# Wider token-major products in a two-block transformer kernel: 512-column blocks, smaller weight granules, other buffer counts

## The chip, the cores and the metric

The kernel runs on one core of a Trainium2 chip. The metric is the device time in microseconds of one execution. Times are medians of several runs of the same program. One further execution was recorded by the hardware profiler; durations and waits in this document come from it.

## The reference

Two residual blocks over 1024 tokens of width 1024, in float32, one after the other. Cut to its products:

```python
# first block
proj = rmsnorm(x) @ w_in                    # 1024 x 9216: a_u, a_v, a_gate, q, k, v, b_gate, gates
y_a  = chunked_spatial_gating(gelu(a_u), gelu(a_v), ...) * silu(a_gate)
y_b  = dilated_attention(q, k, v) * silu(b_gate)
x    = rmsnorm(x + (g_a * (y_a @ w_proj_a) + g_b * (y_b @ w_proj_b)) @ w_out)
# second block, two layers
h = h + rms(ssd_scan(conv(u @ m_in ...)) * silu(z)) * y_g @ m_out     # Mamba-2 mixer, 2048 inner
h = h + (p_0 @ ple_proj) * sigmoid(rmsnorm(h) @ ple_gate)             # gated embedding
h = h + (stick_breaking_attention(q, k, v) * silu(gate)) @ s_out
h = h + (p_1 @ ple_proj) * sigmoid(rmsnorm(h) @ ple_gate)
```

## The kernel before

**Precision and layout.** Every large product is made of three float32r products: each operand is split into a rounded high part and a remainder, and hi x hi, hi x lo and lo x hi are summed in PSUM (`mm`, line 521). The activation of a stage lies transposed, channels on partitions, in an `Act` region (`act1`, `act2`). Its 1024 tokens are 8 token tiles of 128 (`NT`), its 1024 channels 8 channel tiles (`KT`).

**Two kinds of product.** `gemm_b` (line 548) is channel-major: a 128 x 128 tile of the weights is stationary and 512 tokens move; the result has output channels on partitions. `gemm_a` (line 587) is token-major: a 128 x 128 tile of the activation is stationary and the weights move; the result has tokens on partitions. The token-major products are the v projection of the first block (`av`, in `branch_a`), its output projection (`wo`, in `merge`), the four z products of the scan (`z`, in `mamba`), the two halves of the scan's output product (`mo`, in `mamba_out`), the two halves of the last output product (`so`, in `stick_out`) and, in a loop of its own, the gated embedding (`ple`, line 1932, twice), which multiplies each token tile by 8 channel tiles of the gate weights and 2 of the projection.

In `gemm_a` the columns are cut in blocks. For each block, for each token tile, for each channel tile k there are three matmuls into one PSUM bank; then the tile is evacuated by a function of the stage (`ev`, `ev_h`, `ev0`, `ev1`, `evz`).

**Weights.** `Job` (line 344) cuts a weight matrix into granules of 1024 elements per partition, 512 KB each: kind "a" 4 channel tiles x 256 columns, kind "b" 8 x 128, kind "c" 2 x 512. All granules of the kernel stand in one list in order of use. `Weights.loads` (line 383) loads each into a raw slot when one is free. `Weights.splits` (line 396) then takes a split slot, multiplies the granule on GpSimd by a gain where a norm's gain is folded in (`mo`, `ple`'s gate, the products of the second attention), makes the high part on ScalarE (on GpSimd once `hi_on_pool` is set, near the end of the second attention) and the remainder on GpSimd, and gives back the raw slot. A block gives back its split slots after its last token tile. `limit` (line 420) sets how many split and raw slots are in use: there are five split slots and two raw ones in all; a stage that needs the memory for something else uses fewer (four split at first, two in the attentions, there with one raw slot in the second). `taken` (line 969) raises the limit when a region has been given back. At the end `mamba_out` and `stick_out` add two more split slots (offsets 140 and 148).

**Order.** Streams of work (Python generators) are interleaved by a planner, `Sched` (line 245), that keeps an estimated clock of PE and of the other engines, and steps the stream of highest priority that is due. The result is a fixed order of instructions on every engine and DMA queue; at run time each engine follows its own order and waits on semaphores. A granule's ScalarE and GpSimd instructions stand in those queues at the place where the planner put them. All loads and stores are issued from SyncE's queue.

**Memory.** SBUF is one arena, cut by `CUTS` (line 73) into blocks that hold either float32 or float32r. Offsets are in KB per partition; names such as m24r or m172f in the profile give the block's offset and its kind.

**Other buffers that the change touches.** `partial` (line 1851) writes the first half of an output product to DRAM in pieces of 256 columns; `residual` adds them back. `evz` (line 1551) evacuates z with a Tanh on ScalarE and one vector operation, and stores it. `stick_out` hands out the loads of the residual in `begin_turn` (line 2159), one every `TURN[1]` tiles from tile `TURN[0]`.

## Time and profile before

| what | value |
|---|---|
| time, median of 3 runs | 3258.47 us (3257.03 to 3262.03) |
| the profiled execution's own time | 3255.16 us |
| its span in the profile | 3253.4 us |
| PE (TensorE) busy | 3102.3 us, 18830 matmuls |
| VectorE, ScalarE, GpSimd busy | 1725.7, 1404.9, 1257.3 us |
| HBM traffic | 89 GB/s over the span |

PE is the matmul engine, PEld its weight loads, DVE is VectorE, ACT ScalarE, POOL GpSimd, SP SyncE, on whose queue the DMAs are issued. Matmuls overlap, so that a matmul's own duration is longer than the distance between two of them; the distance is read from the starts in the timeline. "Idle before ... <- X" gives the time that an engine waited and the work that released it. L522 is the matmul in `mm`, L533 a transpose, L484 an ACT activation, L488 and L499 vector operations, L507 and L511 GpSimd operations: all are helpers, so the tiles' names tell the stage.

### The profile page before, as it was taken

What the parts mean: (1) busy time and instruction counts of PE and PEld (TensorE: products, weight loads), DVE (VectorE), ACT (ScalarE), POOL (GpSimd) and SP (SyncE); (2) the same over time, 40 slices, a digit from 0 to 9 for tenths busy, and PEclk for the clock granted to TensorE, in tenths of its full rate; (3) what the DMA queues carried; (4) which work ended last, traced back from release to release, by engine and by line L of the source; (5) the groups of instructions that cost most, each with busy time, mean ns of one, the idle gap of its engine ahead of it and who ended that gap; (6) DMA issues with size and microseconds to landing.
All of it is one profiled execution on the core that took longest, in us unless ns stands there. A gap on an engine that the chain in (4) does not pass through costs nothing. (4 is left out here: it accounts for less than half of the span.)

```text
span 3253.4 us, 47763 instructions
## 1 busy us (share of the span) xinstructions
PE 3102.3 (95%) x18830; PEld 2742.4 (84%) x18830; DVE 1725.7 (53%) x3080; ACT 1404.9 (43%) x2569; POOL 1257.3 (39%) x772
## 2 busy tenths in 40 slices
PE   8999999999999999999999989999998989998999
PEld 8988888888888789987878788899977778877899
DVE  2111146667673321567676765443457776878642
ACT  4322255556564311433232323223456766776421
POOL 3332111111112433324445454643335566657750
PEclk9999999999999999999999999999998999999999
DMA  4122221212122753322434334451201111113611
GB/s 138 52 68 78 81 68 57 63 53 59 53 66 91 258 175 130 113 74 77 113 83 114 81 102 146 137 205 40 85 22 33 41 38 40 40 41 120 238 55 52
DMA packets 296052, 291.33 MB, mean 90 GB/s; under 512 B 15556, under 2 KB 252276, under 8 KB 295828
## 3 DMA queue, kind: packets, MB, share of 16 engines
q1 hardware_dynamic: 295828, 288.29, 28.7%
q8 instruction: 147, 2.41, 0.3%
q14 instruction: 77, 0.63, 0.1%
HBM read 216.80 MB, written 71.43 MB: 89 GB/s over the span
## 5 line engine op out<-in xcount | busy, mean ns | idle before, releaser
L507 POOL TENSOR_TENSOR m8r<-m0f,m8r 128x1024 fp32r<-128x1024 f32 (+1 forms) x68 | 163.4, 2403 | 473.8 <-ACT m8r L484 419.1
L507 POOL TENSOR_TENSOR m16r<-m0f,m16r 128x1024 fp32r<-128x1024 f32 x66 | 167.0, 2530 | 440.6 <-ACT m16r L484 401.6
L488 DVE TENSOR_TENSOR m156r<-psum,m156r 128x384 fp32r<-128x384 f32 (+2 forms) x376 | 223.6, 605 | 157.9 <-ACT m156r L484 155.7
L484 ACT ACTIVATE m156r<-psum 128x384 fp32r<-128x384 f32 (+2 forms) x376 | 195.9, 534 | 197.1 <-PE psum L533 184.4
L507 POOL TENSOR_TENSOR m172f<-m172f,m24f 128x127 f32<-128x127 f32 (+7 forms) x128 | 185.0, 1455 | 155.8 <-DVE m24f L2039 106.1
L507 POOL TENSOR_TENSOR m24r<-m0f,m24r 128x1024 fp32r<-128x1024 f32 x64 | 155.8, 2438 | 215.6 <-ACT m24r L484 213.1
L2039 DVE TENSOR_TENSOR_SCAN m24f<-m24f,zero 128x128 f32<-128x128 f32 (+7 forms) x128 | 222.6, 1753 | 8.4 <-ACT m24f L484 7.9
L533 PE MATMUL psum<-ident,m172f 128*128 128x128 f32 (+1 forms) x1314 | 206.4, 280 | 21.5 <-DVE m172f L493 8.5
L499 DVE SCALAR_TENSOR_TENSOR m172f<-m172f,psum 128x256 f32<-128x256 f32 (+1 forms) x112 | 59.5, 534 | 267.8 <-ACT m172f L484 221.6
L533 PEld LDWEIGHTS psum<-ident,m172f 128*128 128x128 f32 (+1 forms) x1314 | 156.9, 144 | 41.4 <-DVE m172f L493 10.2
L484 ACT ACTIVATE m192f<-psum 64x256 f32<-64x256 f32 (+2 forms) x237 | 103.8, 438 | 199.6 <-PE psum L522 128.7
L507 POOL TENSOR_TENSOR smalls<-smalls,mhalf 128x1 f32<-128x1 f32 (+1 forms) x104 | 89.5, 864 | 163.9 <-DVE smalls L495 163.1
L522 PE MATMUL psum<-m108r 128*128 128x512 f32 (+3 forms) x384 | 141.7, 371 | 6.6 <-ACT m172f L484 4.5
L484 ACT ACTIVATE m40f<-psum 128x256 f32<-128x256 f32 (+1 forms) x150 | 66.5, 444 | 181.6 <-PE psum L522 141.6
L507 POOL TENSOR_TENSOR m0f<-m0f,cols 128x1024 f32<-128x1024 f32 x64 | 132.6, 2073 | 31.0 <-DMA m0f<-in_ple_gate_dram 12.6
L493 DVE TENSOR_SCALAR m172f<-m172f,smalls 128x512 f32<-128x512 f32 (+7 forms) x160 | 130.3, 814 | 19.7 <-POOL smalls L507 14.6
L1410 DVE CUSTOM_DVE_ANT_0 m172f<-psum,m24f 128x512 f32<-128x512 f32 (+1 forms) x192 | 102.8, 554 | 65.0 <-PE psum L522 64.8
L1418 ACT ACTIVATE m172f<-m172f,smalls 128x128 f32<-128x128 f32 (+7 forms) x128 | 99.3, 776 | 82.8 <-DVE smalls L495 81.2
L522 PE MATMUL psum<-m60r,m16r 128*128 128x512 f32 x504 | 134.8, 399 | 0.0
L522 PE MATMUL psum<-m44r,m8r 128*128 128x512 f32 x504 | 133.7, 399 | 0.7 <-DVE m108r L499 0.7
L522 PE MATMUL psum<-m60r,m8r 128*128 128x512 f32 x504 | 132.3, 397 | 1.7 <-DVE m108r L499 1.7
L522 PE MATMUL psum<-m44r,m16r 128*128 128x512 f32 x504 | 133.2, 402 | 0.0
(374 smaller groups left out, 8024.5 us busy)
## 6 DMA issues: line engine op xcount, KB each, us to landing
m0f<-in_w_in_dram SPq DMA_DIRECT2D x72, 512.0 KB, 3.8
m0f<-in_m_in_dram SPq DMA_DIRECT2D x38, 512.0 KB, 4.1
m92f<-acum SPq DMA_DIRECT2D x21, 512.0 KB, 10.4
m24f<-in_alibi_dram SPq DMA_DIRECT2D x16, 512.0 KB, 4.2
zd<-m40f SPq DMA_DIRECT2D x64, 128.0 KB, 1.9
m172f<-zd SPq DMA_DIRECT2D x32, 256.0 KB, 9.8
yd<-m172f SPq DMA_DIRECT2D x32, 256.0 KB, 2.2
m0f<-in_m_out_dram SPq DMA_DIRECT2D x16, 512.0 KB
```

Source lines behind the costliest of these rows:

```text
L484: self.nc.scalar.activation(out, in_, func, **k)
L488: self.nc.vector.tensor_tensor(out, a, b, op=op)
L493: self.nc.vector.tensor_scalar(out, a, s1, None, op0=op0)
L499: self.nc.vector.scalar_tensor_tensor(out, a, s, b, op0=op0, op1=op1)
L507: self.nc.gpsimd.tensor_tensor(out, a, b, op=op)
L522: self.nc.tensor.matmul(out, l, r, start=start, stop=stop)
L533: self.nc.tensor.transpose(out, in_, self.ident[:in_.shape[0], :in_.shape[0]])
L1410: nc.vector.tensor_tensor_reduce(row[:, k0:k0 + w], bank[:, :w], Tt[:, off + k0:off + k0 + w], 1.0, -3e38, op0=ALU.add, op1=ALU.max, accum ...
L1418: nc.scalar.activation(row[:, :n], row[:, :n], AF.Exp, bias=nm, accum_out=l)
L2039: nc.vector.tensor_tensor_scan(x[:, ::-1], x[:, ::-1], self.zero.to_broadcast([P, n]), 1.0, op0=ALU.mult, op1=ALU.add)
```

## The change

Token-major blocks become 512 columns wide, made of four granules of 2 channel tiles x 512 columns (kind "a"). The first z product, which carries 32 extra columns, keeps the old shape under the name "n". A split slot is given back as soon as the last token tile has used the granule, not at the end of the block. `ple` goes over 512 columns at a time and waits for each granule where it is first used. There is a sixth split slot (offset 200; 192 becomes the last) and a third raw slot (offset 208, a new cut of the arena); `limit` uses three raw slots unless told otherwise, the merge and the scan use five split slots and not four, the scan's output product six and not five. Evacuations, pieces and stores are 512 columns wide, with two slots where there were four of half the size; `TURN` is halved.

```diff
-    CUTS = (0, 8, 16, 24, 40, 44, 60, 76, 92, 108, 140, 156, 172, 192, 200, 216)
+    CUTS = (0, 8, 16, 24, 40, 44, 60, 76, 92, 108, 140, 156, 172, 192, 200, 208, 216)
...
-        nk, nc = {"a": (4, 256), "b": (KT, P), "c": (2, 512)}[kind]
+        nk, nc = {"n": (4, 256), "a": (2, 512), "b": (KT, P), "c": (2, 512)}[kind]
...
-    def limit(self, n, m=2):
+    def limit(self, n, m=3):
...
-        def products(gs, bank, t, ks):
+        def products(gs, bank, t, ks, over=False):
...
                 e = self.mm(ps, xl, g.hi[:, j, :], False, k == job.kt - 1)
+                if over and j == g.nk - 1:
+                    self.W.release(g)
             return e
...
-                e = yield from products(gs, bank, t, range(job.kt))
+                over = t == NT - 1
+                e = yield from products(gs, bank, t, range(job.kt), over)
...
-            for g in gs:
-                self.W.release(g)
...
-        self.W = Weights(self, self.res(0, 4, 2), Res([self.region(o, 8, "r") for o in (8, 16, 24, 32, 192)]))
+        self.W = Weights(self, Res([self.region(o, 4) for o in (0, 4, 208)]), Res([self.region(o, 8, "r") for o in (8, 16, 24, 32, 200, 192)]))
...
-                J["z", 0] = Job(self, m, 0, 512, "a", more=(5120, 32))
+                J["z", 0] = Job(self, m, 0, 512, "n", more=(5120, 32))
...
-                      go=self.taken(self.r2, 4))
+                      go=self.taken(self.r2, 5))
...
-        zo = self.res(40, 1, 4)
+        zo = self.res(40, 2, 2)
...
-        self.fill_y(self.act1, 1, self.res(172, 4, 3), [self.taken(self.r1, 5)] * NT)
-        ev0, begin, hp_tok = self.partial(self.hp, self.res(40, 1, 4))
+        self.fill_y(self.act1, 1, self.res(172, 4, 3), [self.taken(self.r1, 6)] * NT)
+        ev0, begin, hp_tok = self.partial(self.hp, self.res(40, 2, 2))
...
-        for cb in range(0, D, 256):
-            gs, (gp,) = self.J["pg", i, cb].blocks[0], self.J["pp", i, cb // 512 * 512].blocks[0]
-            pc = slice(cb % 512, cb % 512 + 256)
-            yield ([g.ready for g in gs], gp.ready)
+        for cb in range(0, D, 512):
+            gs, (gp,) = self.J["pg", i, cb].blocks[0], self.J["pp", i, cb].blocks[0]
...
-                    yield act.wait(k // 4, t * P, P)
+                    yield (act.wait(k // 4, t * P, P), gs[k // 2].ready)
...
+                    if j and t == NT - 1:
+                        self.W.release(g)
...
-    TURN = (16, 2)
+    TURN = (8, 1)
...
-        nj, es, half = self.res(172, 4, 2), self.res(188, 1, 4), {}
-        pact = self.embed(1, 156, es, self.weighed)
+        nj, es, half = self.res(172, 4, 2), Res([self.region(o, 2) for o in (188, 190, 212, 214)]), {}
+        pact = self.embed(1, 156, self.res(188, 1, 4), self.weighed)
```

## Rows read from the trace of the kernel before

**Rows 1.** The page's busy table and its 40 slices.
```profile
span 3253.4 us, 47763 instructions
...
PE 3102.3 (95%) x18830; PEld 2742.4 (84%) x18830; DVE 1725.7 (53%) x3080; ACT 1404.9 (43%) x2569; POOL 1257.3 (39%) x772
...
PE   8999999999999999999999989999998989998999
...
PEclk9999999999999999999999999999998999999999
```

**Rows 2.** Windows by stage: stretch, length, busy by engine, granted clock, DMA share, GB/s.
```profile
12.00:113.00 101.00, 99.15 (x801) 98.20 (x802) 25.91 (x44) 42.09 (x79) 29.32 (x22) 1.00 0.27 86
...
1252.00:1344.00 92.00, 92.00 (x770) 92.00 (x769) 26.33 (x54) 20.89 (x31) 24.30 (x18) 1.00 0.31 107
...
1400.00:1973.00 573.00, 531.33 (x3024) 453.80 (x3024) 393.99 (x572) 198.54 (x325) 272.03 (x179) 0.96 0.36 97
1973.00:2119.00 146.00, 132.65 (x1022) 123.43 (x1021) 67.11 (x123) 42.34 (x86) 76.46 (x56) 0.99 0.46 139
2119.00:2215.00 96.00, 93.05 (x781) 92.58 (x780) 41.19 (x65) 25.61 (x42) 44.89 (x21) 1.00 0.50 171
2215.00:2348.00 133.00, 131.76 (x1107) 131.56 (x1106) 53.62 (x100) 45.59 (x81) 43.82 (x30) 1.00 0.19 64
...
2981.00:3063.00 82.00, 75.95 (x583) 72.85 (x582) 57.50 (x65) 46.23 (x103) 65.86 (x45) 0.97 0.55 187
3063.00:3128.00 65.00, 57.47 (x435) 55.50 (x436) 35.98 (x65) 14.26 (x31) 42.48 (x30) 0.92 0.52 174
3128.00:3253.00 125.00, 119.24 (x994) 118.63 (x992) 39.58 (x78) 21.41 (x44) 25.62 (x17) 1.00 0.13 47
```

**Rows 3.** Timeline of PE, v projection: start, length, operation, count.
```profile
62.27 1.60 PE L522 MATMUL psum<-m24r,m60r 128*128 128x256 f32 x12
...
69.47 1.60 PE L522 MATMUL psum<-m24r,m92r 128*128 128x256 f32 x12
```

**Rows 4.** Timeline of PE in a channel-major product.
```profile
1243.80 2.88 PE L522 MATMUL psum<-m76r,m8r 128*128 128x512 f32 x12
...
1249.24 2.88 PE L522 MATMUL psum<-m92r,m8r 128*128 128x512 f32 x12
```

**Rows 5.** Groups by shape, POOL and ACT: count, busy us, mean ns, idle before.
```profile
L507 POOL TENSOR_TENSOR m8r<-m0f,m8r 128x1024 fp32r<-128x1024 f32 x67 | 161.3, 2408 | 472.6 <-ACT m8r L484 417.9 <-PE psum L533 52.4 <-PE psum L522 1.8
...
L507 POOL TENSOR_TENSOR m0f<-m0f,cols 128x1024 f32<-128x1024 f32 x64 | 132.6, 2073 | 31.0 <-DMA m0f<-in_ple_gate_dram 12.6 <-DMA m0f<-in_m_out_dram 11.2 <-DMA m0f<-in_s_in_dram 7.1
...
L484 ACT ACTIVATE m8r<-m0f 128x1024 fp32r<-128x1024 f32 x62 | 65.5, 1057 | 64.0 <-PE psum L522 37.3 <-POOL m0f L507 12.4 <-issue 11.5
```

**Rows 6.** Timeline of PE where the scan's output product passes to its second half.
```profile
2110.36 0.66 PE L533 MATMUL psum<-ident,m172f 128*128 128x128 f32 x4 [3.07 <-DVE m44r L488]
...
2127.50 0.63 PE L533 MATMUL psum<-ident,m172f 128*128 128x128 f32 x4 [1.60 <-DMA m172f<-yd]
```

**Rows 7.** Timeline of PE and POOL around the last output product.
```profile
3027.61 2.32 PE L522 MATMUL psum<-m8r,m44r 128*128 128x256 f32 x18
...
3036.12 1.24 PE L522 MATMUL psum<-m8r,m60r 128*128 128x256 f32 x9
...
3038.96 1.06 POOL L511 TENSOR_SCALAR m140r<-m0f 128x1024 fp32r<-128x1024 f32 x1 [3.12 <-DMA m0f<-in_s_out_dram]
...
3086.48 0.50 PE L522 MATMUL psum<-m140r,m92r 128*128 128x256 f32 x2 [2.44 <-POOL m92r L511]
```

**Rows 8.** Timeline of PE just after the second z product.
```profile
1618.52 3.06 PE L522 MATMUL psum<-m108r,m16r 128*128 128x512 f32 x12 [1.28 <-DVE m40f L499]
```

**Rows 9.** Groups by shape, DVE.
```profile
L499 DVE SCALAR_TENSOR_TENSOR m172f<-m172f,psum 128x512 f32<-128x512 f32 x48 | 32.6, 685 | 120.6 <-ACT m172f L484 74.4 <-DMA m172f<-ga 26.7 <-DMA m172f<-gb 10.5
...
L499 DVE SCALAR_TENSOR_TENSOR m172f<-m172f,psum 128x256 f32<-128x256 f32 x64 | 27.0, 421 | 147.2 <-ACT m172f L484 147.2
```

**Rows 10.** Windows, the first 20 us.
```profile
0.00:20.00 20.00, 8.82 (x38) 7.90 (x39) 6.26 (x10) 9.96 (x16) 8.05 (x16) 1.00 0.80 268
```

More of the change, by code (lines that the diff above doesn't have):

```diff
@@ L615, in gemm_a @@
                     e = yield from products(gs, bank, t, (job.kt - 1,))
+                    if t == NT - 1:
+                        for g in gs:
+                            self.W.release(g)
                     if begin is not None:
@@ L1102, in ev_h @@
         def ev_h(cb, t, ps, e):
-            sl = slice(cb * 256, cb * 256 + 256)
+            sl = slice(cb * 512, cb * 512 + 512)
             return self.Vtt(h[t][:, sl], h[t][:, sl], ps, ALU.add, max(e, he[t]))
@@ L1518, in mamba @@
         xdr, ytr, xer, t2r, str_ = (self.res(o, 2, n) for o, n in ((180, 2), (184, 2), (188, 1), (190, 1), (192, 2)))
-        str_.slots = str_.slots + [self.region(208, 2)]
+        str_.slots = str_.slots + [self.region(212, 2)]
         cbr = self.res(196, 1, 2)
-        zo = self.res(40, 1, 4)
+        zo = self.res(40, 2, 2)
         wr, ar, kr = self.region(180, 4), self.region(184, 4), self.region(188, 2)
@@ L1571, in ev @@
                         s.spawn(1, tables(r))
-                e = self.A(o, ps[:, :256], AF.Tanh, e, scale=0.5)
-                e = self.Vstt(o, o, 1.0, ps[:, :256], ALU.add, ALU.mult, e)
+                e = self.A(o, ps[:, :n], AF.Tanh, e, scale=0.5)
+                e = self.Vstt(o, o, 1.0, ps[:, :n], ALU.add, ALU.mult, e)
                 s.spawn(4, store(cb, t, o, e))
@@ L1819, in ev1 @@
         def ev1(cb, t, ps, e):
-            sl = slice(cb * 256, cb * 256 + 256)
+            sl = slice(cb * 512, cb * 512 + 512)
             return self.Vtt(h[t][:, sl], h[t][:, sl], ps, ALU.add, max(e, he[t].t))
@@ L1846, in fin2 @@
             s.spawn(1, plain(t, e))
-        yield from self.ple(0, self.act1, pact, h, half, self.res(172, 1, 4), fin2)
+        yield from self.ple(0, self.act1, pact, h, half, Res([self.region(o, 2) for o in (172, 174, 212, 214)]), fin2)
         pr.give(s.now)
@@ L1868, in store @@
             yield e
[L1869 removed]
+            d = self.dma(dst[t * P:(t + 1) * P, cb * 512:cb * 512 + 512], o, e)
             pieces.put(o, d)
[L1871 removed]
+            if cb == 1:
                 toks[t].t = d
@@ L1934, in ple @@
         s = self.s
-        for cb in range(0, D, 256):
-            gs, (gp,) = self.J["pg", i, cb].blocks[0], self.J["pp", i, cb // 512 * 512].blocks[0]
-            pc = slice(cb % 512, cb % 512 + 256)
-            yield ([g.ready for g in gs], gp.ready)
-            sl = slice(cb, cb + 256)
+        for cb in range(0, D, 512):
+            gs, (gp,) = self.J["pg", i, cb].blocks[0], self.J["pp", i, cb].blocks[0]
+            sl = slice(cb, cb + 512)
             for t in range(NT):
-                yield (self.px, pact.wait(0, t * P, P))
+                yield (self.px, pact.wait(0, t * P, P), gp.ready)
                 bp = self.px.get()
@@ L1963, in ple @@
                 es.put(x, e)
-                if cb + 256 == D:
+                if cb + 512 == D:
                     fin(t, e)
-            for g in (*gs, gp) if cb % 512 else gs:
-                self.W.release(g)
     def stick(self):
```

47 lines of the change are left out of this document (25 added, 22 removed).

## The prediction

> **What bounds the kernel now.** I read the page's busy table and slices first: TensorE (PE) is busy 95% of a span of 3253.4 us and no slice is much emptier than the others, at a clock granted at full nearly throughout [rows 1]. So the time is the length of PE's queue plus some 151 us in which it sat idle (3253.4 - 3102.3). Then the windows by stage, cut where the timeline of PE passes from one product to the next [rows 2]. The reader is to see which of the stages that the change touches are full: the v projection (12 to 113 us), the output projection of the first block (1252 to 1344), and the gated embedding (2215 to 2348, and 3128 on) leave PE idle for 0 to 2 us each, apart from the last stage's end. The scan (1400 to 1973) has 41.7 us of idle in 573, the first half of its output product (1973 to 2119) 13.4 in 146, the second half (2119 to 2215) 3.0 in 96, and the last output product (2981 to 3128) 13.6. In the full stages a shorter PE queue is a shorter kernel. In the others it is worth less.
>
> Then the timeline of PE inside two full stretches, which prices an instruction. Groups of 12 products 256 columns wide begin 1.44 us apart, 7.20 us for 60 instructions, 120.0 ns each [rows 3]. Groups of 12 that are 512 wide begin 2.72 us apart, 5.44 us for 24, 226.7 ns each [rows 4]. The difference for 256 more columns is 106.7 ns; each instruction carries a further 13.3 ns that does not depend on its width.
>
> **The change, part by part.**
>
> *Wider products.* Two products of 256 columns become one of 512: 2 x 120.0 - 226.7 = 13.3 ns saved a pair. Counting pairs (token tiles x blocks x channel tiles x 3): v projection 8 x 2 x 8 x 3 = 384; output projection 384; the last three z products 3 x 192 = 576 (the first keeps its old shape); scan output 768; gated embedding twice, with its two-channel-tile projection, 2 x (384 + 96) = 960; last output product 384. Together 3456 pairs, 46.1 us, by stage 5.1, 5.1, 7.7, 10.2, 6.4 twice and 5.1. The trace has no product of this form at 512 columns (those in rows 4 have the weights stationary, these have them moving), so the price is bounded by 226.7 and 240.0; I take 226.7, because at 256 columns the moving operand is already a weight and the spacing is that of the same line through both widths. The Trainium skill, page "TensorE: Matmul & The Clock Gate", section "Back-to-back issue gap", gives an isolated product N/2.4 + 2.5 ns, which would make a pair worth only 2.5 ns, all pairs 8.6 us, and the sum below a loss of 8.3. The trace disagrees: 13.3 ns is measured between its two widths.
>
> *Granules of two channel tiles.* A granule stays 512 KB and its preparation stays: ACT's rounded copy 1.06 us, POOL's remainder 2.41, and before both, where a gain is folded in, POOL's product with the gain, 2.07 [rows 5]. What moves is when it must be there. A block of 512 columns needs four granules in its first token tile, where a block of 256 needed two, and it holds four split slots, not two. They come free one by one in the last token tile (8 x 3 products of 226.7 ns, 5.44 us): after 1.36, 2.72, 4.08 and 5.44. The next block wants its granules at 5.44, 6.80, 8.16 and 9.52, from the start of that last tile. Where slots beyond the four are few, POOL's queue decides, one granule every 2.4 us, or 5.7 with a gain (2.07 + 1.06 + 2.41 + two hand-overs of about 0.1, since the remainder waits for ACT and the next gain product is queued behind it). Stage by stage:
> - v projection, four slots, nothing ready ahead: first granule at 1.36 + 1.06 + 2.41 + 0.2 = 5.0, the fourth at 12.2 against 9.5. Loss 2.7 us, and nothing else in the PE queue to cover it.
> - Output projection, five slots now (four before): last granule 9.9 against 9.5. Loss 0.4.
> - Scan output, its first boundary (near 2045): five slots, because the sixth is granted only when the scan gives its region back. One granule is ready ahead; the others, with gain, come at 5.0, 10.7 and 16.4 against 6.8, 8.2 and 9.5. Loss 6.9 us of the main stream. At 2107 to 2128 PE now waits for the scan's y tiles in any case, 3.1 and 1.6 us in two of the waits [rows 6]; a later main stream eats those. I count 3.0. Second boundary, six slots: 1.2. From there eight slots hold two blocks: 0, and likewise in the first gated embedding.
> - Last output product: its blocks take two granules now. Until the scores are done only two split slots and one raw slot exist; the first slot beyond them is written at 3038.96 [rows 7]. Before, the third block began at 3027.61 on one granule. Now the second block begins there and wants two; the raw slot lets the second be loaded only after the first is split (3.5 us on POOL, 4 us of load, 3.5 us again), so it is ready near 3039. The products lost between are 57 (those from the first to the second of PE's rows there, both counted) x 120 ns = 6.8 us, up to 12, which is the whole stretch to 3039, with the wait around them. Against that, PE now idles 7.5 us at 3063 to 3128, waiting for the last remainders of the attention output [rows 2, 7], and there the same 512-column block gives it more to do ahead of the wait. I take a loss of 5 from bounds of 12 and -3.
>
> *Scan stage.* The 7.7 us of the z products are not all path: after each z product PE waits for DVE's evacuation to free a bank, by 1.3 us in the row shown [rows 8], and DVE's queue keeps its length but for 24 instructions fewer. I take half, loss 3.8, bounds 0 and 7.7. The stores of z and of the partial product go from four slots of 256 columns to two of 512, each held over 5.44 us tiles and not 2.88: the same slack, cost nothing, covered by the products of the next tile.
>
> *Evacuations.* Half as many instructions on ACT and DVE, each longer: 0.69 us for 512 columns against 0.42 for 256 [rows 9]. They stand beside PE except behind the very last tile, where a Tanh and two vector operations follow it: some 0.27 us more each, loss 0.8. In the last stage the store of 512 KB at the end is unchanged.
>
> *Third raw slot.* It loads a third granule at the start, ahead of x tiles: 512 KB at the 268 GB/s of that stretch is bounded by 2.0 us later x tiles. Against it, PE was busy for only 8.8 of the first 20 us [rows 10], and a 512-column first tile lets it do up to 2.5 us more products there. I take 0. The residual loads of the last product are handed out every tile from the eighth, not every second from the sixteenth: the same moments, 0.
>
> *Sum.* 46.0 - (2.7 + 0.4 + 3.0 + 1.2 + 5.0 + 3.8 + 0.8 = 16.9) = 29.1 us, on an execution that took 3255.2: 3226.1. The median of the runs lies 3.3 above that execution, so **3229**.
>
> **The rivals.**
> - *All of it arrives.* Stalls at boundaries fall into PE's idle time or into other streams' work, which the kernel has in the scan and the attention tail [rows 2]. 3258.5 - 46.0 = 3212. Against: the v projection has no such work. 0.18.
> - *The first tile of each block is late throughout.* No idle time absorbs anything, the z products give nothing, the last output product loses 12: 46.0 - (2.7 + 0.4 + 7.7 + 6.9 + 1.2 + 12 + 0.8) = 14.3, and with 3 us for the fourth gate granule of the last stage, which has one raw slot until its predecessor ends, 11.3: 3247. 0.22, of which 0.04 reach no difference.
> - *Slower: the gain chain is exposed.* Place: the eight blocks with a gain (four in the scan output, four in the two embeddings). If no granule is ahead, the fourth is ready at 5.0 + 3 x 5.7 = 22.1 against 9.5, 12.6 us a block. It decides from the fourth such block (50 against 46); five give 3258.5 - 46.0 + 63 = 3275. For it: POOL's order is fixed and other work stands in it. Against: eight slots from 2119 on, and POOL busy only 45 of 96 us and 44 of 133 there [rows 2]. 0.04.
> - *Slower: the width is worth nothing.* A product with moving weights at 512 columns takes 240 ns after all, the change does not do what the count says, and the 16.9 us of stalls stand alone: 3275. Against: rows 3 and 4 lie on one line through the columns. 0.03. The rule of the Trainium skill's page on TensorE cited above lies close to this case, with 3267 as an estimate from its 2.5 ns; it shares this chance.
>
> **How the numbers follow.** My sum has 0.53. About 0.2%, 6.5 us, is what a measurement of this kernel can tell from no change. Faster: 0.53 + 0.18 + 0.18 = 0.89; same 0.04; slower 0.07. The range runs from just under the full saving, 3211, to just over the stalls' case, 3248.
>
> **What would show it.** Products 512 columns wide near 226 ns apart at 60 to 100 us, and PE's instructions fewer by 3456. A gap of 2 to 3 us before the v projection's second block, on POOL's remainder. The embeddings shorter by 6 us each with no gap. Wrong would be: PE idle time growing by over 30 us; a wait on POOL's remainders at most boundaries; or the stage at 2981 to 3128 longer than its 147 us.

## The result and the profile after

The changed kernel takes 3230.56 us (median of 4 runs, 3225.63 to 3230.79); the kernel before took 3257.75 us in the same session (median of 4, 3256.37 to 3262.03). The ratio is 0.9911 [0.9894, 0.9928], 27 us faster. Forecast were 3229 us and a range of 3211 to 3248. Two executions of kernels further down, of 9260 and 5386 us, were disturbed and are in no median or ratio.

The page's busy line, and the granted clock, after; of before only the clock, whose busy line is in [rows 1]:

```profile
span 3228.9 us, 40412 instructions
...
PE 3065.7 (95%) x15374; PEld 2556.2 (79%) x15374; DVE 1670.1 (52%) x2944; ACT 1386.8 (43%) x2465; POOL 1268.7 (39%) x772
...
core 0: 3228.9 us, clock 0.978
```
```profile
core 0: 3253.4 us, clock 0.982
```

The count is right to the instruction: 18830 - 15374 = 3456 matmuls fewer. PE's busy time fell by 36.6 us, not by the 46.1 that 13.3 ns a pair make, and its idle time rose from 151.1 to 163.2. The two clock rows say where part of the difference is: 3253.4 x 0.018 = 59 us of full-speed time withheld before, 3228.9 x 0.022 = 71 after. That is one execution of each kernel. In others of the kernel before the clock lay between 0.979 and 0.985, which makes some 49 to 68 us, and what is withheld while PE waits costs nothing; so the 12 us between the two are not all lost, and part of them may be scatter.

The windows of the changed kernel, cut where PE passes from one product to the next (length; busy time and count by engine; granted clock, DMA share, GB/s), and below them the two of before that were not cut so in [rows 2], the scan and the first half of its output product:

```profile
12.49:117.60 105.11, 99.59 (x451) 80.82 (x451) 27.60 (x47) 41.65 (x67) 27.42 (x23) 0.98 0.23 75
117.60:1253.74 1136.14, 1118.74 (x5633) 946.40 (x5632) 494.91 (x1217) 487.47 (x884) 259.39 (x124) 0.99 0.29 92
1253.74:1399.85 146.11, 143.71 (x833) 127.01 (x832) 52.70 (x88) 44.57 (x77) 36.64 (x29) 1.00 0.32 109
1399.85:1944.28 544.43, 514.95 (x2417) 414.32 (x2415) 374.28 (x544) 189.77 (x294) 267.38 (x177) 0.97 0.37 99
1944.28:2105.54 161.26, 140.01 (x697) 111.17 (x696) 78.87 (x134) 48.09 (x83) 82.51 (x59) 0.95 0.46 139
2105.54:2323.55 218.01, 213.36 (x994) 176.12 (x992) 74.38 (x111) 64.06 (x101) 89.38 (x51) 0.99 0.32 108
2323.55:3102.38 778.83, 720.65 (x3866) 606.87 (x3865) 538.11 (x764) 490.73 (x934) 462.44 (x278) 0.97 0.21 66
3102.38:3228.90 126.52, 112.70 (x489) 91.89 (x487) 27.82 (x39) 14.34 (x23) 38.57 (x24) 0.95 0.16 58
```
```profile
1400.37:1969.46 569.09, 527.42 (x2992) 449.89 (x2991) 391.12 (x568) 195.56 (x321) 270.34 (x178) 0.96 0.36 96
1969.46:2119.60 150.14, 136.79 (x1058) 127.57 (x1057) 70.58 (x127) 45.84 (x92) 78.14 (x57) 0.99 0.47 142
```

Set against the prediction's terms, stage by stage (us; all of before cut at the same places):

| stage | before | after | forecast gain | gain |
|---|---|---|---|---|
| v projection | 104.5 | 105.1 | 2.4 | -0.6 |
| first attention and merge | 1135.0 | 1136.1 | 0 | -1.2 |
| output projection, first z | 148.4 | 146.1 | 4.7 | 2.3 |
| scan | 569.1 | 544.4 | 3.9 | 24.7 |
| its output product, first half | 150.1 | 161.3 | 2.1 | -11.1 |
| second half, first embedding | 228.6 | 218.0 | 10.3 | 10.6 |
| second attention, last output product | 779.8 | 778.8 | 0.1 | 0.9 |
| last embedding | 125.4 | 126.5 | 5.6 | -1.1 |
| sum | | | 29.1 | 24.5 |

The sum is near, the parts are not. One stage brought six times its forecast, and three lost where a gain was forecast.

**The price of a product.** PE's timeline in the v projection after:

```profile
114.88 2.88 PE L523 MATMUL psum<-m24r,m92r 128*128 128x512 f32 x12
117.60 2.88 PE L523 MATMUL psum<-m44r,m8r 128*128 128x512 f32 x12
```

Twelve products with moving weights take 117.60 - 114.88 = 2.72 us, 226.7 ns each, as taken from [rows 4].

**The v projection's boundary.** PE's waits in the first tile of its second block, all on POOL's remainders, 2.3 us together:

```profile
73.24 1.43 PE L523 MATMUL psum<-m16r,m44r 128*128 128x512 f32 x5 [0.64 <-POOL m16r L508]
...
75.58 1.66 PE L523 MATMUL psum<-m24r,m76r 128*128 128x512 f32 x6 [0.68 <-POOL m24r L508]
78.25 1.42 PE L523 MATMUL psum<-m24r,m76r 128*128 128x512 f32 x5 [1.02 <-POOL m24r L508]
```

**The scan.** The view of one tile, the slot m40f into which z is evacuated, in the scan's window: who waited for it, before and after.

```profile
L499 DVE SCALAR_TENSOR_TENSOR m40f<-m40f,psum x49: 404/410/422, 1401.2 to 1952.3; 128x256 f32<-128x256 f32 x49
...
who waited for it (us, times):
...
  PE psum L522: 12.8, 7
```
```profile
L500 DVE SCALAR_TENSOR_TENSOR m40f<-m40f,psum x25: 422/681/691, 1401.6 to 1920.3; 128x512 f32<-128x512 f32 x24, 128x256 f32<-128x256 f32 x1
...
who waited for it (us, times):
  DVE m40f L500: 6.9, 9
```

Before, PE waited seven times, 12.8 us, for a PSUM bank that z's evacuation still held. After, never. The scan's idle time fell by 12.2 us (41.7 to 29.5), its busy time by 12.5, of which the products' 7.7 are a part.

**The output product's first half.** PE's waits at its first boundary, and the window behind them:

```profile
2022.59 0.75 PE L523 MATMUL psum<-m200r,m108r 128*128 128x512 f32 x1 [3.17 <-ACT m200r L485]
2026.63 2.50 PE L523 MATMUL psum<-m200r,m108r 128*128 128x512 f32 x5 [3.29 <-POOL m200r L508]
...
2037.27 1.12 PE L523 MATMUL psum<-m172f,m192f 128*128 128x512 f32 x2 [2.11 <-POOL m172f L508]
...
2044.37 2.08 PE L523 MATMUL psum<-m192f,m76f 128*128 128x512 f32 x2 [4.25 <-DVE m192f L489]
...
2024.00:2028.00 4.00, 1.37 (x3) 1.16 (x4) 2.56 (x1) 0.00 (x0) 4.00 (x3) 0.50 0.07 27
```

The first two are the second granule of the second block (m200r), late by 6.5 us. POOL's timeline around it:

```profile
2018.24 0.93 POOL L508 TENSOR_TENSOR smalls<-smalls,mhalf 128x1 f32<-128x1 f32 x1 [4.64 <-DVE smalls L496]
...
2019.40 2.05 POOL L508 TENSOR_TENSOR m0f<-m0f,cols 128x1024 f32<-128x1024 f32 x1
2021.41 2.35 POOL L508 TENSOR_TENSOR m92f<-m92f,m192f 128x1024 f32<-128x1024 f32 x1
...
2024.24 2.33 POOL L508 TENSOR_TENSOR m200r<-m0f,m200r 128x1024 fp32r<-128x1024 f32 x1
```

The granule's load was issued at 1949.35 and landed at 1954.47, but its product with the gain begins only at 2019.40, behind a scan operation for which POOL itself had waited 4.64 us, and another scan operation stands between it and the remainder. From there POOL is busy almost without a pause until 2041; what makes the granule late is its place in POOL's queue, not the amount of work alone. The third wait is for a scan tile that stands behind granules in that queue (POOL's operation at 2036.17). The fourth is VectorE's: it had waited 7.90 us, until 2042.07, for a load into m92f that was issued at 2032.56, as PE ended the products that read that slot, which had come after the first two waits. From 2024 to 2028 the granted clock is 0.50, the 1.2 GHz level, behind two waits with one product between them. The stage's idle time grew by 7.9 us (13.35 to 21.25) and its busy time by 3.2, though it should have lost 5.1.

**The last embedding.** PE's waits in its first tile, and POOL's products with the gain for three of the four granules of its first block:

```profile
3108.72 1.43 PE L523 MATMUL psum<-m140r,m76r 128*128 128x512 f32 x5 [0.97 <-POOL m140r L508]
3115.75 0.79 PE L523 MATMUL psum<-m24r,m76r 128*128 128x512 f32 x1 [5.60 <-POOL m24r L512]
3118.18 2.08 PE L523 MATMUL psum<-m24r,m76r 128*128 128x512 f32 x4 [1.64 <-POOL m24r L508]
```
```profile
3081.84 1.89 POOL L508 TENSOR_TENSOR m0f<-m0f,cols 128x1024 f32<-128x1024 f32 x1 [7.33 <-DMA m0f<-in_ple_gate_dram]
3092.51 1.90 POOL L508 TENSOR_TENSOR m0f<-m0f,cols 128x1024 f32<-128x1024 f32 x1 [3.36 <-DMA m0f<-in_ple_gate_dram]
...
3112.67 1.89 POOL L508 TENSOR_TENSOR m0f<-m0f,cols 128x1024 f32<-128x1024 f32 x1 [3.48 <-DMA m0f<-in_ple_gate_dram]
```

All go through the one raw slot m0f, and POOL idles before each for its load: 10 us a granule, where the prediction had 5.7. The fourth is ready some 16 us after the block began, and PE waits 8.2 us in all.

### The profile page after: what moved, and what is told of

Same layout as the page of the kernel before. It is cut to its first block, busy times and chain, and to the rows that moved or that the text cites. A ratio compares the mean times of both kernels' runs of the same rounds, so it can differ in the third digit from the quotient of the medians.

```text
span 3228.9 us, 40412 instructions
## 1 busy us (share of the span) xinstructions
PE 3065.7 (95%) x15374; PEld 2556.2 (79%) x15374; DVE 1670.1 (52%) x2944; ACT 1386.8 (43%) x2465; POOL 1268.7 (39%) x772
## 5 line engine op out<-in xcount | busy, mean ns | idle before, releaser
L489 DVE TENSOR_TENSOR m156r<-psum,m156r 128x384 fp32r<-128x384 f32 (+2 forms) x376 | 223.4, 605 | 146.7 <-ACT m156r L485 144.7
L508 POOL TENSOR_TENSOR m8r<-m0f,m8r 128x1024 fp32r<-128x1024 f32 x46 | 112.8, 2451 | 295.1 <-ACT m8r L485 290.3
L508 POOL TENSOR_TENSOR m16r<-m0f,m16r 128x1024 fp32r<-128x1024 f32 (+1 forms) x47 | 119.9, 2551 | 271.7 <-ACT m16r L485 221.6
L2045 DVE TENSOR_TENSOR_SCAN m24f<-m24f,zero 128x128 f32<-128x128 f32 (+7 forms) x128 | 206.8, 1630 | 7.1 <-ACT m24f L485 6.7
L534 PEld LDWEIGHTS psum<-ident,m172f 128*128 128x128 f32 (+1 forms) x1314 | 158.9, 144 | 45.6 <-POOL m172f L508 10.2
L523 PE MATMUL psum<-m200r,m108r 128*128 128x512 f32 (+1 forms) x480 | 150.1, 393 | 6.5 <-POOL m200r L508 3.3
L508 POOL TENSOR_TENSOR m24r<-m0f,m24r 128x1024 fp32r<-128x1024 f32 (+1 forms) x40 | 100.9, 2524 | 135.5 <-ACT m24r L485 135.1
L500 DVE SCALAR_TENSOR_TENSOR m172f<-m172f,psum 128x512 f32<-128x512 f32 x64 | 43.7, 686 | 188.2 <-ACT m172f L485 144.1
L523 PE MATMUL psum<-m76r,m8r 128*128 128x512 f32 x504 | 132.7, 397 | 0.0
```

The costliest lines, as they stand in the source:

```text
L489: self.nc.vector.tensor_tensor(out, a, b, op=op)
L500: self.nc.vector.scalar_tensor_tensor(out, a, s, b, op0=op0, op1=op1)
L508: self.nc.gpsimd.tensor_tensor(out, a, b, op=op)
L523: self.nc.tensor.matmul(out, l, r, start=start, stop=stop)
L534: self.nc.tensor.transpose(out, in_, self.ident[:in_.shape[0], :in_.shape[0]])
L2045: nc.vector.tensor_tensor_scan(x[:, ::-1], x[:, ::-1], self.zero.to_broadcast([P, n]), 1.0, op0=ALU.mult, op1=ALU.add)
```

## The experiments

All are edits of the changed kernel, and ratios are to the kernel before (the changed one has 0.9911). The planner works out the order of all instructions anew for each, so a stage can move a little without being edited: in the eight kernels that leave it as changed (the changed one is one of them), the scan took 541.4 to 548.3 us. Only stages that move by more are read.

### The v projection

```diff
-        J["av"] = Job(self, w, D, D, "a")
+        J["av"] = Job(self, w, D, D, "n")
...
-            return self.A(v[:, t, cb * 512:(cb + 1) * 512], ps, AF.Gelu_apprx_tanh, e)
+            return self.A(v[:, t, cb * 256:(cb + 1) * 256], ps, AF.Gelu_apprx_tanh, e)
```


> Only the v projection goes back to blocks of 256 columns. In the changed kernel this stage (first product at 12.5 us to the next stage's first at 117.6) is as long as before the change, 105.1 us against 104.5, although it has 384 pairs fewer. Theory: the width is worth 13.3 ns a pair, 5.1 us, and it is given back in the stage itself: some 2.6 us because the first tile of the first block waits for granules, and 3.2 us because the second block does. Narrow, the stage comes out at 104.5 (+-0.5) and the kernel within 1 us of the changed one. Rival: the width is worth nothing in this product and the stalls are absorbed later; then the narrow stage loses both stalls and is about 99 us, the kernel 5 us faster. Rival 2: the stalls are not of this width at all (they come from the third raw slot); then the narrow stage keeps them and is 110 us.

Measured: 3231.64 us, 0.9922 [0.9909, 0.9935], the changed kernel's time. The stage takes 106.0 us, so the width gains 0.9 there and not 5.1, and the narrow form with three raw slots is 1.5 us behind the same form with two (104.5). The first 20 us show part of that; the windows of the changed kernel and of the one with two raw slots (below):

```profile
0.00:20.00 20.00, 7.50 (x27) 5.86 (x28) 5.32 (x8) 9.11 (x13) 9.86 (x16) 0.98 0.83 292
```
```profile
0.00:20.00 20.00, 8.49 (x28) 6.28 (x28) 6.17 (x10) 9.87 (x16) 8.07 (x16) 1.00 0.79 269
```

With three slots PE is busy 7.50 us of the first 20 against 8.49 with two: the third load delays x (its third tile lands at 13.43 us against 12.00), a loss of about 1 us.

```diff
-        self.limit(4)
+        self.limit(5)
```


> Five split slots instead of four from the start on; nothing else. Theory: the second block of the v projection waits 2.3 us in its first tile and 0.9 in the next because its granules come from POOL at 2.4 us apiece with none ahead; with one ahead the last is late by 0.4, so these waits go to under 1 us and the stage (105.1 us) is 2 to 3 us shorter, plus what the clock loses behind the waits (nothing is seen of it there). The kernel is 2 to 3 us faster, at the edge of what can be measured. Rival: the third raw slot, not the split slots, is what is late (the last granule's load comes only when a raw slot is given back): the waits stay, 0 us.

Measured: 3210.67 us, 0.9866 [0.9850, 0.9883]: 15 us or so under the changed kernel, far more than expected. The stage did as expected, 103.1 us, and its waits at the second block are gone. But the first attention is 6 us shorter as well (1130.1), and the stretch from the second attention to the end, which was not touched, 8.4 us. The first attention explains why nothing that was lost in the v projection shows: in all twelve kernels with four split slots (the one before, too) the two stages together take 1239.5 to 1241.8 us, whether the v projection takes 104.5 to 106.0, as in ten of them, or, in two below, 108.6 and 111.8. What it loses is given back at the merge, where PE waits in the changed kernel 5.9 us for vector and scalar tiles, 3.0 in the kernel with 108.6 and 0.2 in the one with 111.8. The two longest of these waits in the changed kernel:

```profile
1074.47 0.96 PE L523 MATMUL psum<-m140r,m200r 128*128 128x512 f32 x3 [1.75 <-DVE m140r L489]
...
1081.26 1.94 PE L523 MATMUL psum<-m140r,m200r 128*128 128x512 f32 x3 [3.65 <-ACT m140r L485]
```

With five slots, here and in the last run, the pair takes 1233.2 and 1235.0. Here two thirds of the 8 us come after 908 us, where the waits at the merge are 2.4 us instead of 5.9; what else five slots shorten was not taken apart.

```diff
-    def limit(self, n, m=3):
+    def limit(self, n, m=2):
...
-        W.raw.slots = W.all_raw
+        W.raw.slots = W.all_raw[:2]
```


> Two raw slots instead of three, everywhere; nothing else. Theory: at the start the third granule's 512 KB no longer go ahead of the x tiles, so the first block gets back up to 2 us (the narrow v projection was 1.5 us longer with three slots than the kernel before with two: 106.0 against 104.5); at the second block the same 2 to 4 us of waits stay, since there POOL decides. Later stages within 1 us each, the kernel 0 to 2 us faster. Rival: the third raw slot is what keeps POOL fed at boundaries (load and split would alternate): the v projection's second block and the gated embeddings lose 3 to 6 us each, the kernel 5 to 15 slower.

Measured: 3210.24 us, 0.9863 [0.9835, 0.9891]; both expectations were wrong. The start has its 1 us back, but the v projection is 3.5 us longer (108.6) and the output projection with the first z 3.9 (150.0): there the third slot does feed the boundary (PE idles 4.7 us in the second of these stages instead of 2.4; the v projection's share is given back at the merge). Against this the second half of the output product and the first embedding are 5.1 us shorter and everything from the second attention on 15.0. That last stretch has one raw slot in both kernels up to the last embedding; it is treated under the raw slot.

### The scan

```diff
-                    J["z", g] = Job(self, m, g * 512, 512, "a")
+                    J["z", g] = Job(self, m, g * 512, 512, "n")
...
-                n = 256 if g == 0 else 512
+                n = 256
```


> Only the last three z products go back to 256 columns, 576 pairs; their evacuations and stores with them. In the changed kernel the stretch from the first 512-wide product of the convolution (1399.9 us) to the start of the output product's second half (2105.5) takes 705.7 us, 13.5 less than before, where the prediction had about 5 to 6. Theory A (the prediction's): half of the z products' 7.7 us was path, the stretch goes to 709.5, the kernel +3.8. Theory B: all of it is path, 713.4, +7.7. Theory C: the z products bring the whole surplus, because their fewer evacuations also shorten a queue that the scan waits for: 716 to 719, +10 to +13. Theory D: the scan is bound elsewhere and the z products bring nothing: 705.7 (+-1), and the surplus comes from the output product.

Measured: 3240.49 us, 0.9953 [0.9940, 0.9966], some 14 us slower than the changed kernel. The scan takes 580.0 us, 36 more than in the changed kernel and 11 more than before the change; the stretch from the second attention on gives 12.5 of them back, the output product's first half 6.0. The two store slots of 512 columns now hold 256 each, and ScalarE waits 27.5 us for stores to land. The run mixed two edits, so the next one gives the four slots back on top of this edit.

```diff
-        zo = self.res(40, 2, 2)
+        zo = self.res(40, 1, 4)
```


> The last three z products at 256 columns as in the run before this one, but their stores again go through four slots of 256 columns; there they had two slots of 512, which a narrow product fills by half. Theory: in the kernel before, PE waits in the scan for the vector engine's evacuation of z (8 rows that name that slot, 12.8 us), in the changed kernel in none, so the wide z is worth its 7.7 us of products and some 12 of waits: the scan (1400 to the output product's start) comes out at 566 to 572 us as before the change, where the changed kernel has 544, and the kernel 10 to 20 us slower than the changed one. The first trial's 580 us were due to the two slots, 10 of them. Rival: it is the width alone; the store slots do nothing and the scan takes 580 again. Rival 2: the scan's gain is not z's: 544 to 552.

Measured: 3247.66 us, 0.9973 [0.9961, 0.9984], 20 us slower than the changed kernel; the scan 575.2 us. Its window, and PE's waits for m40f:

```profile
1397.05:1972.25 575.20, 529.30 (x2989) 454.02 (x2987) 383.08 (x568) 195.13 (x319) 271.20 (x181) 0.96 0.36 96
...
  PE psum L523: 9.5, 4
```

The wait for the evacuation is back, and so is the time: the scan's gain is the wide z's. The store slots were worth 5 us in the run before, not 10.

```diff
-                e = self.A(o, ps[:, :n], AF.Tanh, e, scale=0.5)
-                e = self.Vstt(o, o, 1.0, ps[:, :n], ALU.add, ALU.mult, e)
+                m = e
+                for c in range(0, n, 256):
+                    x = self.A(o[:, c:c + 256], ps[:, c:c + 256], AF.Tanh, m, scale=0.5)
+                    e = max(e, self.Vstt(o[:, c:c + 256], o[:, c:c + 256], 1.0, ps[:, c:c + 256], ALU.add, ALU.mult, x))
```


> The changed kernel, with its z products 512 columns wide, but each is evacuated by two Tanh and two products of 256 columns instead of one of 512 (the former shape of the evacuation; 24 of each more). Theory A: the waits went because PE stays 5.44 us in a tile instead of 2.88 while an evacuation holds a bank, whatever its shape: the scan stays at 544 to 549 us. Theory B: the waits went because the vector engine has fewer instructions in its queue: half of the gain or more is lost, the scan takes 553 to 565 us.

Measured: 3231.08 us, 0.9929 [0.9912, 0.9945]. The window of the scan, and who in PE's queues waited for m40f:

```profile
1397.71:1956.91 559.20, 526.07 (x2416) 422.69 (x2415) 371.55 (x568) 190.86 (x318) 266.43 (x177) 0.95 0.36 96
...
  PEld psum L523: 0.5, 1
```

Neither theory stands alone. The waits for the bank stay away (0.5 us), as A says: they went with the time that PE spends in a wide tile. Yet the stage is 14.8 us longer, as B says, and three quarters of that is PE busy for longer (11.1 us) with the same products at a lower clock (0.95 against 0.97). The order is another one, too, and what brought the clock down was not taken apart.

### The output product

```diff
-            J["mo", kh] = Job(self, a["m_out_2"][0], 0, D, "a", k0=kh * KT,
+            J["mo", kh] = Job(self, a["m_out_2"][0], 0, D, "n", k0=kh * KT,
```
with the pieces and evacuations of both halves at 256 columns again.

> Both halves of the scan's output product go back to 256 columns, 768 pairs of 13.3 ns (10.2 us). Theory (the prediction's terms): the first half gives back 5.1 - 3.0 - 1.2 = 0.9 us net, the second 5.1; the kernel is 6 us slower than the changed one, and the stretch up to the second half's start (705.7 us) is about 1 us longer. Theory B: the waits at the first boundary fall into time in which other streams are late anyway, and the pairs count in full: +5.1 in the stretch, +5.1 behind it, the kernel +10. Theory C: the whole surplus of 13.5 us sits in the first half of the output product: stretch 719, kernel +18.

Measured: 3218.77 us, 0.9888 [0.9868, 0.9908]: not 6 to 18 us slower but faster by some 7. The second half and the embedding are 4.7 us longer, as the pairs say (5.1). The first half is 10.2 us shorter narrow:

```profile
1943.53:2094.63 151.10, 137.71 (x1057) 129.13 (x1056) 75.03 (x127) 47.70 (x94) 88.15 (x61) 0.98 0.50 146
```

Against the 161.26 above it has 360 matmuls more, 2.3 us less busy time and 7.9 us less idle time. Narrow, this half took 151.1 to 152.0 us in three kernels; wide with the gain, 155.1 to 163.2 in nine, so the loss depends on the order but its sign does not.

```diff
-                              gain=self.col["ynorm"][:, kh * KT:(kh + 1) * KT])
+                              gain=None if kh == 0 else self.col["ynorm"][:, kh * KT:(kh + 1) * KT])
```


> The changed kernel, with the first half of the scan's output product at 512 columns, but its eight granules without the product with the norm's gain, 2.07 us of POOL each (so the output leaves the gain of these rows out). Theory: this half (1944 to 2106) is 10 us longer wide than narrow because the four granules of its second block come one after another through POOL, gain product and remainder of each between the scan's own work there: waits of 3.17 and 3.29 us on the granule, and 2.11 and 4.25 behind POOL's late scan tiles. Without the gain the waits shrink and the half takes 150 to 154 us, the kernel 7 to 11 faster. Rival: the granules wait for their loads or for split slots, not POOL's work: 158 to 161 us.

Measured: 3196.25 us, 0.9810 [0.9793, 0.9828]. The first half at 512 columns without the gain products:

```profile
1944.89:2082.78 137.89, 132.36 (x672) 106.73 (x670) 71.16 (x127) 42.14 (x74) 65.65 (x50) 0.98 0.45 138
```

16.9 us less POOL work in the stage, and the stage is 23.4 us shorter, 13.2 less than even the narrow form with the gain. The theory's mechanism holds and its size was too small: one wait of 1.4 us on a granule is left, and in this stage POOL's queue, not PE's, sets the time at the boundary, for the granules and for the scan's tiles behind them. The edit also takes a step out of each granule's own chain, which this run does not separate; but that step's 2 us are fewer than the 6.5 that PE waited for one granule. Another 11.7 us of the kernel's gain lie from the second attention on, where nothing was edited.

### Releasing one by one

```diff
-                if over and j == g.nk - 1:
-                    self.W.release(g)
...
                 if fin is not None and cb == last:
                     fin(t, r)
+            for g in gs:
+                self.W.release(g)
```
and the same in the embedding.

> Split slots are given back all at the end of a block instead of one by one in its last token tile; widths and granules as changed. Theory: every boundary at which no granule is ready ahead waits up to 4.1 us longer (the first of four slots comes free at 5.44 us of that tile instead of 1.36): the v projection's by 3 to 4 (105 to 108 or 109), the output projection's by 2 to 4, the scan output's first by 3 to 4, the single z blocks by up to 4 each where the next weights are split late; with clock lost behind these waits, 10 to 20 us in all. Rival: other granules are ahead at most places, so only the v projection loses its 3 to 4 us: within 5 us of the changed kernel.

Measured: 3230.36 us, 0.9922 [0.9900, 0.9944], the changed kernel's time, but not for the rival's reason. The v projection lost 6.7 us (111.8), the second half of the output product with the first embedding 15.0. PE's waits at one of these boundaries, in the embedding's second block:

```profile
2272.39 0.50 PE L523 MATMUL psum<-m16r,m76r 128*128 128x512 f32 x1 [1.51 <-ACT m16r L485]
2274.81 2.50 PE L523 MATMUL psum<-m16r,m76r 128*128 128x512 f32 x5 [1.92 <-POOL m16r L508]
```

The first attention gave back 6.1, the first half of the output product 4.5, the scan 3.6 (as much as its scatter), and the stretch from the second attention to the end 8.4, none of which the edit asked for. So the one-by-one release is worth some 15 us in the embedding and the half before it, and the total hides it.

### The raw slot of the last stage

```diff
         self.W.limit(2, 1)
+        self.W.raw.slots = [self.W.all_raw[0], self.W.all_raw[2]]
```


> A second raw slot of 512 KB from the second attention to the end of the last output product (the arena place that the new third raw slot has, unused there); nothing else. In the changed kernel the last stretch, from the last output product's first product (about 2953) to the end, takes 276 us where 272 were taken before, and the first tile of the last embedding waits 1.0, 5.6 and 1.6 us on the preparation of its granules. Theory: one raw slot makes load and split of these granules alternate, though split slots are free; with two the 8.2 us go to under 2 and the second block of the last output product loses some of its 4.2 us of waits: the last stretch 265 to 269, the kernel 7 to 11 us faster than the changed one. Rival: the granules wait for POOL, which has the softmax's and the heads' remainders in its queue, so the stall stays or moves: 0 to -2 us. Rival 2: the earlier loads take DMA time from the second attention's own tiles: slower there by some us.

Measured: 3219.09 us, 0.9886 [0.9872, 0.9899]. The last embedding takes 115.6 us instead of 126.5, without the waits; POOL's gain products there begin earlier and alternate between two slots:

```profile
3065.51 1.90 POOL L508 TENSOR_TENSOR m0f<-m0f,cols 128x1024 f32<-128x1024 f32 x1
3076.61 2.87 POOL L508 TENSOR_TENSOR m208f<-m208f,cols 128x1024 f32<-128x1024 f32 x1
```

That is the theory's figure, but it must be read with the other runs. With one raw slot the last embedding took 120.8 to 126.6 us in six kernels of ten, and 115.5 to 116.6 with no such wait in four (five split slots, late release, two raw slots, and the one without the gain in the output product). POOL's timeline in the kernel with five split slots, and in the changed one:

```profile
3039.29 2.40 POOL L508 TENSOR_TENSOR m24r<-m0f,m24r 128x1024 fp32r<-128x1024 f32 x1
3046.83 1.05 POOL L512 TENSOR_SCALAR m8r<-m0f 128x1024 fp32r<-128x1024 f32 x1 [5.15 <-DMA m0f<-in_ple_proj_dram]
...
3058.02 1.90 POOL L508 TENSOR_TENSOR m0f<-m0f,cols 128x1024 f32<-128x1024 f32 x1 [0.98 <-DMA m0f<-in_ple_gate_dram]
```
```profile
3062.35 2.41 POOL L508 TENSOR_TENSOR m24r<-m0f,m24r 128x1024 fp32r<-128x1024 f32 x1
...
3070.14 1.06 POOL L512 TENSOR_SCALAR m8r<-m0f 128x1024 fp32r<-128x1024 f32 x1 [2.38 <-DMA m0f<-in_ple_proj_dram]
```

The first gate granule starts 37 us ahead of the embedding in the one (3058.02 against 3095.45) and 20.5 in the other (3081.84 against 3102.38). At 10 us a granule, 37 are enough for four and 20.5 are not. The ten kernels with one raw slot part in the same way: without the wait the first gate granule starts 28.0 to 37.4 us ahead, with it 20.5 to 25.2. The lateness comes from further up the same chain: from the remainder of the output product's last granule (m24r) to the first gate granule it is 18.7 us in the one and 19.5 in the other, but that remainder stands 56 us ahead of the embedding in the one and 40 in the other. Why it came later there was not taken apart. From the second attention to the end the changed kernel took 905.3 us, the longest of the changed form; the nine others of the changed form without the second raw slot took 890 to 903, 896 in the mean, and three with the second raw slot 884 to 892, 888 in the mean. So the second raw slot takes the wait away in any order (three runs of three), and is worth about 8 us against the mean order; the rest was the order that the changed kernel happened to get.

### What beats both

```diff
-            J["mo", kh] = Job(self, a["m_out_2"][0], 0, D, "a", k0=kh * KT,
+            J["mo", kh] = Job(self, a["m_out_2"][0], 0, D, "na"[kh], k0=kh * KT,
...
+        self.W.raw.slots = [self.W.all_raw[0], self.W.all_raw[2]]
```
with the pieces of the first half at 256 columns.

> Two edits of the changed kernel together: the first half of the scan's output product alone at 256 columns (its second half stays at 512), and the second raw slot from the second attention on. Theory: the first half is 10 us shorter narrow (151 against 161), because its two boundaries at 512 columns wait for granules with a gain (8 us more idle time) and the granted clock falls behind the waits (0.95 against 0.98 to 0.99); the second half keeps its 5 us; the raw slot brings 10 to 11 at the last embedding. They stand in different stages, so they add: 20 us under the changed kernel, about 3209 us. Rival: what is saved in the first half is lost again where the second attention waits for other things: 3219, as with the raw slot alone.

Measured: 3204.38 us, 0.9844 [0.9829, 0.9860]. The first half takes 151.5 us and the last embedding 115.5, so both savings arrive, and the rival's 3219 is excluded; the sum is 5 us below the expected 3209, about what the second attention is shorter by (6 us), which no edit asked for.

The same with five split slots from the start:

> The changed kernel with three edits: five split slots from the start, the first half of the scan's output product at 256 columns, and the second raw slot in the second attention. Theory: they stand in different stages and add. Measured one by one by stage: v projection and first attention together 8 us shorter with five slots (1233 against 1241), the output product's first half 10 (151.5 against 161.3), the last embedding 11 (115.5 against 126.5): 3228.9 - 29 = 3200 of span, and near 3196 if the second attention stays as in the run with the last two edits (772.7). Rival: the order of instructions is worked out anew for each kernel, and part of what five slots brought in the first attention and all that one raw slot already had in some runs (115.6 at the last embedding with five slots alone) is luck of that order: then no better than the last two edits alone, 3204 (+-3).

Measured: 3195.53 us, 0.9815 [0.9802, 0.9829], span 3191.1: 35 us under the changed kernel, 62 under the one before. The theory's 3200 and 3196 were spans, 5 to 9 us above the measured one; the rival, no better than the run before, is excluded. The two first stages take 1235.0 us, the first half 152.0, the last embedding 115.5. Of the 13.8 us of span below the run without five slots, 6.4 are the two first stages'; 4.0 in the last stretch and 3.9 in the scan are no larger than their scatter.

## Why the prediction was right, and where it was not

The total was right by luck: the scan brought 21 us more than forecast, the first half of its output product 13 less, the last embedding 7, the v projection 3 and the output projection 2 less, and these errors nearly cancel. What holds is the price of a product.

- *Wider products.* 13.3 ns a pair and 3456 pairs: shown, by the spacing of 226.7 ns, and where PE is full by the second half of the output product with the first embedding (10.6 us gained of 11.5) and by the second half's return to narrow (4.7 of 5.1). The Trainium skill, page "TensorE: Matmul & The Clock Gate", section "Back-to-back issue gap", gives an isolated product N/2.4 + 2.5 ns, as an estimate 215.8 ns at 512 columns. The trace has 226.7 in this stream of products, and the measurement decides.
- *Scan: "I take half, loss 3.8, bounds 0 and 7.7".* The failed step, by 21 us. The prediction read one wait of 1.3 us [rows 8] as a reason why PE's saving might be lost, and bounded the gain by the products. The seven waits add up to 12.8 us and they vanish with the width: a wide tile gives the evacuation of the one before 5.44 us instead of 2.88. The bound had to be the products plus the waits, 20.5. The other 4 us are busy time, at a mean clock of 0.97 instead of 0.96; they were not taken apart and are as large as the scan's scatter.
- *First boundary of the scan's output product: "Loss 6.9 us of the main stream ... I count 3.0".* The failed step on the other side. 6.5 us of waits on one granule were seen, but their likeness to 6.9 is chance. The prediction had the three granules that are not ahead finished 5.0, 10.7 and 16.4 us after the start of the last tile, so that the last of them would be late. From 2011.91, where that tile starts, they took 14.7, 20.2 and 27.6, and PE waited for the first. The prediction had POOL begin a granule as soon as its slot is free; in the trace the granule has a fixed place in POOL's queue, among the scan's operations and their waits. The 5.0 also holds no product with the gain; with its 2.07 us behind the taking of the slot, as the program orders it, the prediction's own sum would be 7.1, 12.8 and 18.5, a loss of 9.0. Nor did anything later absorb the waits: scan tiles came late behind them and the clock fell, and the stage lost 11 us instead of gaining 2. The rival that had this term at 6.9 was still too mild.
- *Last embedding.* The sum forecast 6.4 less 0.8 with no stall, and only a rival had the one raw slot, at 3 us. It cost 8.2 in waits. The 5.7 us a granule left out the load, which with one slot cannot overlap: 10 us.
- *v projection: "In the full stages a shorter PE queue is a shorter kernel".* The boundary's loss was right (2.3 us of waits on POOL's remainders, forecast 2.7), and the third raw slot cost about 1 at the start. But twelve kernels show that with four split slots what is lost here, up to 6.7 us, does not reach the merge's end; that a gain would not reach it either is not shown. The prediction did not ask whether the first attention held slack, because the v projection itself showed no idle time.
- *Output projection with the first z.* 2.3 of 4.7, with 2.4 us of idle time where there was 0.3; not taken further.
- *Last output product: "a loss of 5 from bounds of 12 and -3".* The stretch with the second attention gained 0.9, forecast 0.1. It scatters by 12 us with the order, so this is no confirmation.
- *The clock.* The prediction called it full nearly throughout and gave it no term. In the profiled executions it withheld 12 us more than before, not all of it lost.

Of the signs named, the spacing, the count, the gap ahead of the v projection's second block and the first embedding (5.9 us shorter, 122.7 to 116.8) came as forecast; the last embedding did not. Of the signs of being wrong, PE's idle time grew by 12 us and not by 30. The last output product took 148.0 us instead of 146.7, within the 146 to 155 that it takes over the kernels. Waits on POOL's remainders did come at many boundaries: the v projection's, those of both halves of the scan's output product, the last output product's and the last embedding's.

## What to carry to other kernels

Where PE waits for a bank that an evacuation holds, add those waits to what a wider tile saves, since they can go with it; where four granules are due in a tile instead of two, price each by everything that it passes through in series (load if there is one raw slot, gain, copy, remainder) and count what else stands in that queue and what the queue itself waits for. Before a stage's saving is booked, see whether the next meeting of streams has idle time: a full stage can still be followed by slack. In a kernel whose order is planned, an edit moves things that it does not touch, so read each by its stage, and take an unedited stage's scatter over several kernels as the measure.

## What was not expected of the hardware

A wait of some 3 us can cost more than itself: behind the waits at 2022 to 2027 the granted clock stood at 0.50, and five products of 512 columns took 2.30 us (2026.63 to 2028.93), 460 ns each instead of 227. Not every such wait does: before the change PE waited 3.07 us at 2110.36 [rows 6], and from 2108 to 2116 the granted clock was 1.00. In the run with two evacuations the same products took 11 us longer in the scan at 0.95 than at 0.97.
